# A mixture of experts in another order of steps: about three experts in flight instead of two

## The chip, the cores and the metric

The kernel runs on one core of one Trainium2 chip. The metric is the device time of one execution in microseconds (us), and the number to be predicted is the median of several runs of the changed kernel.

## The reference, cut to what matters

The program is a chain of two transformer blocks on 256 tokens of width 1024, all in float32. The change touches only the mixture of experts near the end of the second block, of which the reference is:

```python
def moe_swiglu(x, router_w, w1, w3, w2):
    """x: (B,S,D). Top-2 of 8 expert SwiGLU, gates = softmax over the selected logits."""
    ...
    logits = (xt @ router_w).astype(jnp.float32)
    top_vals, top_idx = lax.top_k(logits, TOP_K)
    gates = jax.nn.softmax(top_vals, axis=-1)
    ...
    for e in range(N_EXPERTS):
        out = out + combine[:, e:e + 1] * swiglu(xt, w1[e], w3[e], w2[e])
```

There are 8 experts. w1 and w3 of one expert are 1024 x 3584, its w2 is 3584 x 1024, so that the weights of all experts are 352 MB, and each is needed once. The 256 tokens take two experts each, 64 to an expert on average.

## The kernel before, in words

**Stages.** The attention blocks, a dense feed-forward layer and the router come first, up to about 805 us. Then the experts run until about 1700 us, then a small gated projection ends the kernel.

**Steps.** The hidden width of an expert is cut in four chunks (CHUNKS): three of 1024 columns, c = 0, 1, 2, and one of 512, c = 3. One step is one pair (expert, chunk). ORDER puts the experts as 0, 4, 1, 5, 2, 6, 3, 7, and STEPS sorts the pairs by 2 i + c, where i is the place in ORDER. So a steady stretch repeats chunk 0 of expert i, chunk 2 of expert i - 1, chunk 1 of expert i, chunk 3 of expert i - 1. The order of the weights in memory traffic follows the same list (_moe_steps, weights). A step with c = 0, 1 or 2 is called long below, one with c = 3 short.

**What a step does.** In experts(), each turn of the loop runs the w1 product of its chunk (result in the PSUM banks mm, then Silu to sw_s), its w3 product (banks s, then the product with sw_s), and the w2 product of the step before (banks o, added to the expert's results). A product is a call of wide(). It first does the first 64 tokens of the expert, with matmuls of 128 rows and 64 columns of the array. The tokens 65 to 96 and 97 to 128 (the function rest) are put off until the first weight part of the next product has run (catch_up). They stand under `with self.tc.If(many() > SET):` (line 1507) and a second, inner If (line 1510), so that their matmuls are in the program for every product but are jumped over where the expert has no more than 64 or 96 tokens. A weight part is given back only in rest, whether or not the If was taken.

**Between the parts.** The list mids puts other TensorE work between the parts of the w1 product, late between those of the w3 product:

- hidden, at part 2: transposes sw_s of the step before, for its w2 product (bank pair tr).
- gather, at parts 4 and 5: the inputs of the next expert, in the step just before its chunk 0 (`begin[x] == i + 1`). Its matmuls are tr<-oh,f. They write xT, a tile of inputs_T().
- turn of way_back, at part 6, and the four pieces of scatter at parts 2 to 5 of the w3 product: the results of an expert that has finished go back to its tokens. That is one step after the w2 product of its chunk 3.

**Weights.** _Stream loads weights in parts of 512 KB, in the order of use, from SyncE's queue (line 90). A part is loaded as soon as a slot is free: 8 wp, 10 in pool qp (EARLY), 6 in rp (MORE), 4 wh, 4 wl, 3 x and 1 gain make a ring of 36 slots, all tiles of 128 x 1024 floats. The first time round there are three more.

**Inputs and results.** inputs_T() and results() take their tiles of 512 KB from three buffers each (tags xh and xl of pool act).

Of the kernel before, what the change touches and what calls it, by code (L numbers as in the profile page):

```python
# [19 lines left out]
P = 128  # L20
# [3 lines left out]
KD = D // P  # L24
FF = 3584
FC = FF // 512
NE = 8
# [4 lines left out]
NC = len(CHUNKS)  # L32
# [2 lines left out]
BIG = 3e38  # L35

RAW = 8
EARLY = 10
MORE = 6
PARTS = 4  # L40
LAG = 2
# [5 lines left out]


ORDER = [e for e0 in range(NE // 2) for e in (e0, e0 + NE // 2)]
STEPS = [(ORDER[i], c) for _, c, i in sorted((2 * i + c, c, i) for i in range(NE) for c in range(NC))]  # L50


def _moe_steps():

    prev = None
    for e, c in STEPS:
        yield from (("w1", e, c), ("w3", e, c))
# [122 lines left out]
class _Direct:  # L180


    def __init__(self, net, stream):
        self.net = net
        self.plan = {c[0]: c for c in stream.plan}
        self.slot = (net.qp, "raw", EARLY)
        assert stream.loaded == len(stream.parts) and len(stream.parts) - stream.used <= stream.last
# [20 lines left out]
class _Net:  # L208
# [112 lines left out]
    def split(self, v, j=0, more=False):  # L321

        k, n = v.shape[1], v.shape[2]
        if more:
            wh, wl = (self.t(self.qp, [P, 1024], "raw", bufs=EARLY).bitcast(F32R) for _ in range(2))
        else:
# [1129 lines left out]

        return back, turn

    def inputs_T(self):
        return self.t(self.act, [P, KD, P], "xh", bufs=3)  # L1460

    def gather_tiles(self):
# [115 lines left out]

        self.wide(key, y, lhs, 512, many, take, mids)

    def results(self):
        return self.t(self.act, [P, 2, 512], "xl", bufs=3)

    def scatter(self, t, e, back, ys, many=None):
# [35 lines left out]
    def experts(self, sp, p, pp):  # L1620

        F = lambda f, *x: lambda: f(*x)
        tokens, xT, ys, back, gs = {}, {0: self.xg}, {}, {}, {}
        prev = done = None
        begin = {e: i for i, (e, c) in enumerate(STEPS) if c == 0}

        def number(e):

            if e not in tokens:
                tokens[e] = self.nc.values_load(self.counts[0:1, e : e + 1], engines=(mybir.EngineType.PE,), min_val=0, max_val=S)  # L1630
            return tokens[e]

        def turn_back(e):
            back[e], turn = self.way_back(sp, e)
            turn()

        def hidden_last(e, c, s):
            g = self.t(self.qp, [P, 1024], "raw", bufs=EARLY).rearrange("p (i q n) -> p i q n", i=2, q=4)
            gs[e, c] = self.hidden(sp, s, CHUNKS[c][1] // 2, g)

        def hidden(e, c, s):
            gs[e, c] = self.hidden(sp, s, CHUNKS[c][1] // 2)

        def finish(e, c, mids=None):

            if c == 0:
                ys[e] = self.results()
            self.down(("w2", e, c), ys[e], gs.pop((e, c)), CHUNKS[c][1] // 2, F(number, e), c == 0, mids)
            return e if c == NC - 1 else None

        for i, (e, c) in enumerate(STEPS):
            n = CHUNKS[c][1] // 2
            s = self.t(sp, [P, 2, 512], "sw_s")
            mids, late = {}, {}
            if i == 0:
                mids[2] = [self.begin]
            else:
                mids[2] = [F(hidden, *prev)]
            nx = [x for x in range(NE) if begin[x] == i + 1]
            if nx:  # L1660
                x = nx[0]
                oh = self.places(sp, x)
                xT[x] = self.inputs_T()
                for k in (0, 4):
                    mids.setdefault(4 + k // 4, []).append(F(self.gather, oh, xT[x], k))
            if done is not None:
                back[done], turn = self.way_back(sp, done)
                mids.setdefault(6, []).append(turn)
                late = {2 + 2 * t + k: [f] for t in range(NT) for k, f in enumerate(self.scatter(t, done, back[done], ys[done], F(number, done)))}
            if n < 512:  # L1670
                mids, late = ({k: m.get(2 * k, []) + m.get(2 * k + 1, []) for k in range(4)} for m in (mids, late))
            if i == len(STEPS) - 1:
                late[3] = [F(turn_back, e)]
                self.next_gain()
            self.up(("w1", e, c), xT[e], s, n, F(number, e), True, mids)
            self.up(("w3", e, c), xT[e], s, n, F(number, e), False, late)
            if i < len(STEPS) - 1:
                done = finish(*prev[:2]) if prev is not None else None
            else:
                finish(*prev[:2], {4: [F(hidden_last, e, c, s)]})  # L1680
            prev = (e, c, s)
            if i == len(STEPS) - 3:
                pT = self.ple_T(p)

        self.stream.wait()
        self.stream.advance(2)
        finish(*prev[:2])
        self.stream.advance(4)
        value = self.ple_value(1, pT, pp)
        self.play(value, n=1)  # L1690
        self.catch_up()
        self.sets.pop("s")
        ps = [[self.bank(tag) for _ in range(2)] for tag in ("tr", "s")]
        for t in range(NT):
            self.spread(ps[t], t, back[e], ys[e])
        with self.tc.If(number(e) > SET):
            for t in range(NT):
                self.spread_rare(ps[t], t, back[e], ys[e])
        return value, [F(self.add_gated, t, j, e, ps[t][j]) for t in range(NT) for j in range(2)]
# [153 lines left out]
    def moe(self, i):  # L1853
# [3 lines left out]
        value, done = self.experts(sp, p, pp)  # L1857
        x0, *x0T = (self.t(self.qp, [P, D], "raw", bufs=EARLY) for _ in range(3))
        x0T = [x.bitcast(F32R).rearrange("p (k n) -> p k n", k=KD) for x in x0T]
# [20 lines left out]
    def run(self, stop):  # L1880
# [8 lines left out]
        with ExitStack() as cx:  # L1889
# [7 lines left out]
            if n < stop:  # L1897
                self.qp = cx.enter_context(tc.tile_pool(name="sQ", bufs=1, reuse_waits="tile"))
                self.stream.more(self.qp, EARLY)
                self.mixer(1, *st, self.route_join, more, self.router_inputs)  # L1900
# [82 lines left out]
```

## Time and profile before

| what | value |
|---|---|
| median of 3 runs | 1743.54 us |
| lowest and highest | 1737.5 and 1758.56 us |
| the profiled execution | 1751.32 us |
| its span, first to last instruction | 1749.5 us |
| mean granted TensorE clock | 0.977 of full speed |
| TensorE (PE) busy | 1645.0 us, 94% |
| VectorE, ScalarE, GpSimd busy | 676.7, 513.9, 157.8 us |
| read from HBM | 486.60 MB |

The profiled execution is one run with the hardware profiler. What it spends outside its span is 1.8 us. All durations in the rows come from it, and the median of the runs lies 7.8 us under it. A busy PE is not a PE at its peak, since matmuls overlap.

### The profile page before, as it was taken

The numbers are of one execution on the slowest core, as the hardware profiler recorded it, in microseconds if no ns is written. First come the engines' busy times: TensorE is split into PE (matmuls) and PEld (weight loads), VectorE is DVE, ScalarE is ACT, GpSimd is POOL, SyncE is SP. The second block draws the span as 40 slices with busy tenths as digits, with TensorE's granted clock in tenths as the row PEclk, the third lists the DMA queues.
The fourth block names the chain that finished last, engine by engine and source line by source line (L and its number), as shares of the span: only waits on it lengthen the run. The fifth ranks groups of instructions, "written<-read, shape, count | busy, mean of one in ns | idle before, by whom it ended". The sixth has DMA issues, their size and how long they took to land. (4 is left out here: it accounts for less than half of the span.)

```text
span 1749.5 us, 24548 instructions
## 1 busy us (share of the span) xinstructions
PE 1645.0 (94%) x9749; PEld 1017.8 (58%) x9749; DVE 676.7 (39%) x1132; ACT 513.9 (29%) x840; POOL 157.8 (9%) x152
## 2 busy tenths in 40 slices
PE   8999999999999999999999998999998999989787
PEld 6887777787888877785334344345343353333336
DVE  6656767556544577663111201210211212112145
ACT  5646646555444455552000000000000000000013
POOL 2001433501000011420000000000000000000011
PEclk9999999889999999999999999999999999999998
DMA  8664325535555548748999999889999999999981
GB/s 274 199 183 146 111 86 163 193 103 175 177 190 192 192 157 293 235 164 353 406 403 406 406 398 357 341 346 343 348 378 368 377 406 389 401 407 404 402 302 67
DMA packets 176118, 491.71 MB, mean 281 GB/s; under 512 B 16670, under 2 KB 21206, under 8 KB 175920
## 3 DMA queue, kind: packets, MB, share of 16 engines
q1 hardware_dynamic: 171376, 474.28, 73.2%
q0 software_dynamic: 4544, 14.52, 2.8%
q8 instruction: 157, 2.57, 0.6%
q14 instruction: 41, 0.34, 0.1%
HBM read 486.60 MB, written 2.14 MB: 279 GB/s over the span
## 5 line engine op out<-in xcount | busy, mean ns | idle before, releaser
L282 PE MATMUL mm<-wh,xh 128*128 128x512 f32 (+5 forms) x996 | 325.0, 415 | 7.7 <-PEq L1507 2.4
L333 DVE TENSOR_TENSOR wl<-raw,wh 128x1024 fp32r<-128x1024 f32 x211 | 269.0, 1286 | 133.9 <-ACT wh L329 123.0
L282 PE MATMUL mm<-wh,xl 128*128 128x512 f32 (+1 forms) x700 | 279.7, 400 | 0.7 <-DVE xl L504 0.5
L329 ACT CAST wh<-raw 128x1024 fp32r<-128x1024 f32 x226 | 235.4, 1051 | 138.6 <-PE mm L282 67.1
L282 PE MATMUL mm<-wl,xh 128*128 128x512 f32 (+2 forms) x840 | 248.0, 422 | 3.5 <-PEq L1507 2.7
L282 PE MATMUL mm<-raw,xh 128*64 128x512 f32 (+3 forms) x1236 | 184.9, 475 | 13.0 <-PEq L1507 7.3
L1547 DVE TENSOR_TENSOR sw_s<-sw_s,s 128x512 f32<-128x512 f32 (+1 forms) x64 | 39.8, 621 | 402.6 <-PE s L282 366.8
L282 PE MATMUL o<-raw,sw_g 128*64 128x512 f32 (+1 forms) x1132 | 173.8, 501 | 16.0 <-PEq L1507 13.3
L282 PEld LDWEIGHTS mm<-wh,xh 128*128 128x128 f32 (+2 forms) x996 | 147.8, 171 | 54.3 <-issue 14.1
L282 PE MATMUL s<-raw,xh 128*64 128x512 f32 (+3 forms) x1016 | 158.7, 484 | 15.2 <-PEq L1507 6.9
L282 PEld LDWEIGHTS mm<-wl,xh 128*128 128x128 f32 (+2 forms) x840 | 141.1, 181 | 49.4 <-issue 13.5
L282 PEld LDWEIGHTS mm<-wh,xl 128*128 128x128 f32 x700 | 134.0, 191 | 29.5 <-DVE xl L504 2.5
L1560 ACT COPY sw_g<-tr 128x512 f32<-128x512 f32 (+1 forms) x31 | 16.6, 537 | 417.3 <-PE tr L285 417.3
L282 PEld LDWEIGHTS o<-raw,sw_g 128*64 128x64 f32 (+1 forms) x1132 | 64.8, 126 | 114.4 <-issue 74.4
L282 PEld LDWEIGHTS mm<-raw,xh 128*64 128x64 f32 (+1 forms) x1236 | 67.0, 127 | 107.7 <-issue 66.6
L282 PEld LDWEIGHTS s<-raw,xh 128*64 128x64 f32 (+1 forms) x1016 | 61.9, 130 | 104.7 <-issue 74.3
L1545 ACT ACTIVATE sw_s<-mm 128x512 f32<-128x512 f32 (+1 forms) x64 | 34.8, 544 | 198.7 <-PE mm L282 167.2
L1573 DVE TENSOR_TENSOR xl<-xl,o 128x512 f32<-128x512 f32 x48 | 32.9, 686 | 148.6 <-PE o L282 126.7
L310 POOL DMA_DIRECT2D gain<-in_ple_norm_g_dram x2 | 1.1, 558 | 860.0 <-DMA raw<-in_moe_w_dram 859.1
L331 POOL TENSOR_TENSOR wl<-raw,wh 128x1024 fp32r<-128x1024 f32 x15 | 37.9, 2545 | 402.5 <-ACT wh L329 382.5
L282 PE MATMUL s<-wh,xh 128*64 128x512 f32 (+6 forms) x364 | 58.8, 439 | 0.7 <-PEq L1507 0.3
L285 PEld LDWEIGHTS tr<-c_ident,sw_s 128*128 128x128 f32 x280 | 32.9, 147 | 30.8 <-issue 10.5
(387 smaller groups left out, 1786.1 us busy)
## 6 DMA issues: line engine op xcount, KB each, us to landing
raw<-in_moe_w_dram SPq DMA_DIRECT2D x454, 512.0 KB, 10.2
raw<-in_dense_w_dram SPq DMA_DIRECT2D x84, 512.0 KB, 4.5
wh<-in_moe_w_dram SPq DMA_DIRECT2D x72, 512.0 KB, 10.1
wl<-in_moe_w_dram SPq DMA_DIRECT2D x72, 512.0 KB, 10.1
x<-in_moe_w_dram SPq DMA_DIRECT2D x54, 512.0 KB, 10.1
raw<-in_w_in_dram SPq DMA_DIRECT2D x48, 512.0 KB, 4.6
raw<-in_nsa_w_in_dram SPq DMA_DIRECT2D x44, 512.0 KB, 5.1
gain<-in_moe_w_dram SPq DMA_DIRECT2D x17, 512.0 KB, 10.2
```

The lines of the kernel that those rows point to most:

```text
L282: self.nc.tensor.matmul(out, lhsT, rhs, start=start, stop=stop, **kw)
L285: self.nc.tensor.transpose(out, in_, self.ident if ident is None else ident)
L310: (eng or self.nc.gpsimd).dma_start(out, ap.partition_broadcast(P))
L329: self.nc.scalar.copy(wh, v)
L331: self.nc.gpsimd.tensor_tensor(wl, v, wh.bitcast(F32), ALU.subtract)
L333: self.owed.append(lambda: self.nc.vector.tensor_sub(wl, v, wh.bitcast(F32)))
L1545: nc.scalar.activation(s[:, i, :n], ps[i][:, :n], AF.Silu)
L1547: nc.vector.tensor_mul(s[:, i, :n], s[:, i, :n], ps[i][:, :n])
L1560: copy(g[:, i, : n // P, :], ps[:, :n].rearrange("p (q n) -> p q n", n=P))
L1573: self.nc.vector.tensor_add(ys[:, i, :], ys[:, i, :], y[i])
```

## The change

- STEPS sorts by 4 i + 3 c in place of 2 i + c. A steady stretch becomes chunk 0 of expert i, chunk 3 of expert i - 2, chunk 2 of expert i - 1, chunk 1 of expert i. So an expert is spread over ten steps in place of eight, and three are open at a time. The step list before begins (expert, chunk) (0,0) (0,1) (4,0) (0,2) (4,1) (0,3) (1,0) (4,2) (1,1) (4,3) (5,0); after, it begins (0,0) (0,1) (4,0) (0,2) (4,1) (1,0) (0,3) (4,2) (1,1) (5,0) (4,3). The last five steps are the same in both.
- EARLY goes from 10 to 8, so that the ring has 34 slots.
- Every fourth expert in ORDER takes its inputs and results from two new tiles, xh4 and xl4, in pool sE.

```diff
-EARLY = 10
+EARLY = 8
...
-STEPS = [(ORDER[i], c) for _, c, i in sorted((2 * i + c, c, i) for i in range(NE) for c in range(NC))]
+STEPS = [(ORDER[i], c) for _, c, i in sorted((4 * i + 3 * c, c, i) for i in range(NE) for c in range(NC))]
...
-    def inputs_T(self):
+    def inputs_T(self, i=0):
+
+        if i % 4 == 3:
+            return self.t(self.se, [P, KD, P], "xh4")
         return self.t(self.act, [P, KD, P], "xh", bufs=3)
...
-    def results(self):
+    def results(self, i=0):
+        if i % 4 == 3:
+            return self.t(self.se, [P, 2, 512], "xl4")
         return self.t(self.act, [P, 2, 512], "xl", bufs=3)
...
-                ys[e] = self.results()
+                ys[e] = self.results(ORDER.index(e))
...
-                xT[x] = self.inputs_T()
+                xT[x] = self.inputs_T(ORDER.index(x))
```

## Rows read from the trace of the kernel before

**Rows 1.** The page: busy time by engine (part 1), DMA queues (part 3).
```profile
PE 1645.0 (94%) x9749; PEld 1017.8 (58%) x9749; DVE 676.7 (39%) x1132; ACT 513.9 (29%) x840; POOL 157.8 (9%) x152
...
q8 instruction: 157, 2.57, 0.6%
```

**Rows 2.** Busy time by stretch: length, engines, PE clock share, DMA share, GB/s.
```profile
825.00:1060.00 235.00, 226.05 (x1593) 98.29 (x1589) 31.27 (x52) 19.24 (x34) 0.00 (x0) 0.99 1.03 404
1060.00:1450.00 390.00, 360.60 (x2963) 161.58 (x2962) 57.80 (x100) 25.08 (x46) 0.00 (x0) 0.98 0.94 361
1450.00:1675.00 225.00, 202.18 (x1027) 82.42 (x1025) 42.08 (x73) 18.03 (x33) 0.56 (x1) 0.98 1.03 403
```

**Rows 3.** Waits of SyncE's DMA queue, 805 to 1690 us: in total, times, longest.
```profile
SPq L90 <- DMA raw<-in_moe_w_dram: 254.9, 278, 2.0
SPq L90 <- PEq L1507: 116.1, 29, 11.4
```

**Rows 4.** Timeline of SyncE: issues into the one gain slot; the last expert loads.
```profile
902.37 0.33 SPq L90 DMA_DIRECT2D gain<-in_moe_w_dram  x1
...
1603.17 0.33 SPq L90 DMA_DIRECT2D gain<-in_moe_w_dram  x1
...
1675.97 5.34 SPq L90 DMA_DIRECT2D raw<-in_moe_w_dram  x5
```

**Rows 5.** Timeline of PE: the first use of the same tiles; the experts' last product.
```profile
920.36 1.06 PE L282 MATMUL o<-gain,sw_g 128*64 128x512 f32 x4
...
1622.47 1.06 PE L282 MATMUL o<-gain,sw_g 128*64 128x512 f32 x4
...
1697.17 2.79 PE L282 MATMUL o<-raw,raw 128*64 128x512 f32 x12 [0.15 <-PEq L1507]
```

**Rows 6.** DMA issues of the whole run: count, size, us from issue to landing.
```profile
gain<-in_moe_w_dram SPq DMA_DIRECT2D x17, 512.0 KB, 10.2
```

**Rows 7.** Instructions of line 1507: duration ns min/median/max; PE's timeline behind one.
```profile
L1507 PEldq COMPARE_BRANCH  x96: 65/422/7665, 810.3 to 1701.9; - x96
...
1651.56 1.82 PE L282 MATMUL mm<-raw,xh 128*64 128x512 f32 x4 [4.06 <-PEq L1507]
```

**Rows 8.** DMA queue of instructions: packets in 955:1440, 1440:1690 and 1624:1647.
```profile
q8 instruction: 60, 0.98, 0.8%
...
q8 instruction: 39, 0.64, 1.1%
...
q8 instruction: 4, 0.07, 1.2%
```

**Rows 9.** Timeline of PE: where steps start, and the moved work in them.
```profile
820.49 1.06 PE L282 MATMUL mm<-raw,xh 128*64 128x512 f32 x4
...
848.49 1.06 PE L282 MATMUL mm<-raw,xh 128*64 128x512 f32 x4
...
1526.11 1.06 PE L282 MATMUL mm<-x,xh 128*64 128x256 f32 x8
1529.34 3.84 PE L282 MATMUL tr<-oh,f 128*128 128x128 f32 x32
1549.81 1.06 PE L282 MATMUL mm<-raw,xh 128*64 128x512 f32 x4
...
1571.21 1.06 PE L282 MATMUL mm<-x,xh 128*64 128x512 f32 x4
1599.55 1.39 PE L282 MATMUL mm<-raw,xh 128*64 128x512 f32 x4
1624.18 1.06 PE L282 MATMUL mm<-raw,xh 128*64 128x256 f32 x8
1645.84 0.66 PE L285 MATMUL tr<-c_ident,p 128*128 128x128 f32 x4
1646.43 1.08 PE L282 MATMUL mm<-raw,xh 128*64 128x512 f32 x4
```

**Rows 10.** Timeline of PE: some of one product's matmuls for tokens past 64.
```profile
955.50 3.23 PE L282 MATMUL mm<-raw,xh 128*32 128x256 f32 x56
```

## The prediction

> **What bounds the kernel now.** I read the page first. TensorE is busy 94% of the span [rows 1], and no other engine comes near it, so the question is what TensorE waits for among the experts, the only stage that the change touches. Next comes the table by stretches [rows 2]. DMA moves 404 GB/s from 825 to 1060 us and 403 from 1450 to 1675, but 361 from 1060 to 1450, where its share falls to 0.94. The middle stretch holds 390 x (1 - 361/404) = 41.5 us in which DMA had nothing to do. SyncE's waits say why: 254.9 us for a load that is still under way, but also 116.1 us for line 1507, that is for slots that are given back only behind the If [rows 3]. So in the middle the ring is full and TensorE is the slower of the two; at both ends DMA runs without a break.
>
> That looks as if DMA bounded the ends and TensorE the middle, and a better mix would win back the 41.5 us. The next view decides it: does TensorE wait for weights at the ends? The gain tile is one slot of the ring and so a probe every 36 loads. It is issued at 902.37 and 1603.17 [rows 4], lands 10.2 us later [rows 6], and is first used at 920.36 and 1622.47 [rows 5]. The weights lay there for 17.99 - 10.2 = 7.8 us and 19.30 - 10.2 = 9.1 us, and these are the stretches in which the ring is emptiest. The last expert load is issued at 1675.97 + 5.34 = 1681.3 at the latest and lands at about 1691.5; the product that uses it runs from 1697.17. TensorE never runs out of weights. DMA at 404 GB/s is in time, and its idle 41.5 us cost nothing.
>
> What TensorE waits for at the ends is its own program. The compare-and-branch of line 1507 takes 0.07 us at the least and 7.67 at the most, and behind one of them PE stands still for 4.06 us [rows 7]. The instructions come through DMA in packets of 2.57 MB / 157 = 16 KB [rows 1, 8]. From 1440 to 1690 us, where the jumped-over matmuls are read in vain, there is one per 250/39 = 6.4 us; from 955 to 1440, where two experts execute theirs, one per 485/60 = 8.1 us [rows 8]. One expert of those runs both sets of matmuls for tokens past 64, 3.23 us for 56 of the 128 in one product [rows 10]. So a step of a light expert (at most 64 tokens) takes about as long as reading its program, a step of a heavy one as long as its matmuls.
>
> The short step shows it best. From 1624.18 to 1646.43 it takes 22.25 us with four such packets, 5.6 us each [rows 8, 9]. Its w1 and w3 products have half the columns but the same number of instructions as a long step's, so there is free time of TensorE in it.
>
> **The change part by part.** The profiled execution took 1751.3 us, 1.8 of them outside the span; the median of the runs is 7.8 us lower. I add the change to either.
>
> *Two slots fewer.* TensorE's start is not touched: the first loads land long before. DMA falls behind by two loads, 2 x 0.524 MB / 404 GB/s = 2.6 us. The cover is the 7.8 us at the emptiest probe, which leave 5.2. Between probes it can be less; I allow two us. Cost 0; without cover each missing us would cost one.
>
> *Heavy steps in other places.* The expert with two sets is third in ORDER. Its steps are number 7, 9, 12, 14 of 32 before and 6, 9, 12, 15 after; those of the other heavy one 15, 17, 20, 22 and 14, 17, 20, 23. Both kernels execute the same matmuls and read the same program. Heavy steps hardly come more evenly than before, and the DMA idle time stays within some us of 41.5. Cost 0.
>
> *The gather changes its host.* It comes just before a chunk 0. Before, six of the seven gathers sit in a short step (the one for expert 4 stays in step 2). After, these six sit in chunk 1 of the expert before, a long step. What it costs in either host is read from steps of light experts [rows 9]. Short with gather: 1549.81 - 1526.11 = 23.70 us. Short without: 22.25, less the foreign transposes at its end (1646.43 - 1645.84 = 0.59), so 21.66. The gather's 3.84 us of matmuls cost 2.04 there, the rest hides in the reading of the program. Long with gather: 848.49 - 820.49 = 28.00. Long without anything: 1624.18 - 1599.55 = 24.63. It costs 3.37 there, nearly all of it. So each move out of a light short step costs 1.33 us. Four of the six short steps are light; in the two heavy ones the matmuls of the later tokens are executed and the gather costs its whole length in both places. 4 x 1.33 = 5.3 us. Bounds: if the long step hid it all and the short one lost 2.04, -8 us (4 x 2.04); if the long step paid 3.84 six times and the short one gave nothing back, +23 us.
>
> A rule of the skill would give another sum. In the Trainium skill, Runtime: NRT & Kernel Launch, section "Instruction fetch mechanics", crossing into the next 16 KB of program is called mostly hidden, while a taken branch out of the window of two pages stalls. By its first half a short step would be as long as its matmuls, the gather would cost its length anywhere, and this term would be 0 and the time 1743.5, inside the spread of rival A. The four packets in 22.25 us speak against that half here, and the branch of 7.67 us for the other.
>
> *The scatter changes its host.* It comes one step after the w2 product of chunk 3: before in a chunk 2, after in a chunk 1, both long. It costs 1599.55 - 1571.21 = 28.34 us less 24.63, 3.71 in the one [rows 9] and the same in the other: 0. New is that gather, turn and hidden then share one w1 product and the two tr banks. Who is queued behind is the rest of that product. A bank must be copied out before its next user, and each waits at least one weight part. I know no row of the three together; 0 to 0.5 us each, six times, 0 to 3, and I take 0, as the copies run beside weight parts.
>
> *New tiles.* xh4 and xl4 are written once for each of two experts; before, a buffer came round after three experts, now four. No wait is added. Cost 0.
>
> Sum: +5.3 us. 1751.3 + 5.3 = 1756.6 against the profiled execution, 1743.5 + 5.3 = 1749 for the median.
>
> **The rivals.**
>
> A, the forecast: TensorE and its program bound the stage, 1749 us (1737 to 1757 with the spread of steps).
>
> B: a mix of three lets the program's reading run ahead in heavy steps and so shortens the light ones beside them. For it: a packet per 8.1 us where heavy steps run. Against: heavy steps are as many and as far apart as before. A plain long step takes 24.63 us; its three products of 32 matmuls, at 2.79/12 = 0.23 us each [rows 5], are 22.3. If a third of the other 2.3 us vanished in each of the 18 light long steps, -14 us: 1729.
>
> C: I misread the spare weights, and DMA's idle time is what counts. All of it regained, less the two slots: -41.5 + 2.6 = -39, 1705 us. Against: the weights that lie ready for 7.8 us and more at both ends.
>
> D, the other side: gather and scatter stacked in one long step are paid in full, and the short step stays at 23.7 us because four packets take their time whatever stands in it. Then the upper bound holds, +23 us: 1767. It decides for this if short steps without gather last over 23 us. For it: the packets of a step do not depend on the gather. Against: the short step of 22.25 us.
>
> E: the ring runs dry at one end, as 5.2 us of cover prove too few beside other delays; one stall of 6 to 10 us near one of the two probes: 1757 to 1759, say 1758.
>
> That the change does not do what it says, as heavy work lies where it lay, is part of A.
>
> **How the numbers follow.** A 0.62, B 0.15, C 0.04, D 0.14, E 0.05. The likeliest is 1749. The range leaves out C and the far ends of B and D: 1728 to 1768. About 2% is what a measurement of this kernel can tell from no change, its runs alone spread over 1.2%: 35 us, so under 1709 or over 1778. Faster by that: C, 0.04. Slower: D with more behind it, 0.04. Within: 0.92.
>
> **What would show it.** In the profile after, light short steps without gather should take some 22 us, chunk 1 steps with gather and scatter some 31 to 32; the gain tile should still lie ready for about 5 us at the emptiest; DMA between 1060 and 1450 should stay near 361 GB/s and the count of instruction packets at 157. I am wrong if PE waits for loads of moe weights by the tens of us, if the plain long step leaves 24.6, or if DMA's idle time and the time fall together.

## The result, and the profile after

| | before | after |
|---|---|---|
| median of 17 runs each | 1745.65 us | 1754.55 us |
| lowest to highest | 1737.5 to 1758.56 | 1747.69 to 1762.6 |
| the profiled execution (its span) | 1751.32 (1749.5) | 1753.85 (1752.0) |
| mean granted TensorE clock | 0.977 | 0.981 |

The ratio is 1.0064 [1.0047, 1.008]: the new order costs 8 to 14 us. The forecast was 1749, its range 1728 to 1768.

First, the page's rows for TensorE and for the instruction queue, against [rows 1]:

```profile
PE 1638.8 (94%) x9749; PEld 1011.1 (58%) x9749; DVE 674.9 (39%) x1132; ACT 514.3 (29%) x840; POOL 158.1 (9%) x152
...
q8 instruction: 157, 2.57, 0.6%
```

The same matmuls run, and the same 157 packets of program are read. The stretches, against [rows 2] (length, engines, PE clock, DMA share, GB/s):

```profile
825.00:1060.00 235.00, 220.53 (x1549) 92.99 (x1547) 31.46 (x52) 17.72 (x31) 0.00 (x0) 1.00 1.01 398
1060.00:1450.00 390.00, 359.86 (x2906) 161.55 (x2906) 59.04 (x101) 25.71 (x47) 0.00 (x0) 0.98 0.94 362
1450.00:1675.00 225.00, 200.88 (x1094) 83.28 (x1082) 42.78 (x75) 17.44 (x33) 0.56 (x1) 0.96 1.01 396
```

DMA still has idle time in the middle, 362 GB/s after 361. SyncE's waits between 805 and 1690 us say the same as [rows 3]:

```profile
SPq L90 <- DMA raw<-in_moe_w_dram: 261.6, 290, 2.4
SPq L90 <- PEq L1510: 106.1, 30, 10.5
```

Line 1510 is the If that was line 1507 before. The branch and its packets, against [rows 7, 8] (durations in ns; packets from 955 to 1440, then from 1440 to 1690 us):

```profile
L1510 PEldq COMPARE_BRANCH  x96: 65/426/6779, 797.5 to 1699.6; - x96
...
q8 instruction: 62, 1.02, 0.8%
...
q8 instruction: 38, 0.62, 1.0%
```

**Where the time went.** Cut both traces at TensorE's first expert matmul and at its first matmul of the projection behind the experts. In the timeline of PE these are, of the kernel after:

```profile
792.40 1.94 PE L282 MATMUL mm<-raw,xh 128*64 128x512 f32 x8
...
1695.59 0.50 PE L282 MATMUL mm<-wh,xh 128*128 128x512 f32 x1
```

and of the kernel before:

```profile
805.15 1.97 PE L282 MATMUL mm<-raw,xh 128*64 128x512 f32 x8
...
1699.89 0.50 PE L282 MATMUL mm<-wh,xh 128*128 128x512 f32 x1
```

| us | before | after | difference |
|---|---|---|---|
| front, up to the experts | 805.15 | 792.40 | -12.75 |
| stage, the experts | 894.74 | 903.19 | +8.45 |
| tail, behind them | 49.61 | 56.41 | +6.80 |
| span | 1749.5 | 1752.0 | +2.5 |

The front's difference isn't shown to be the change's: other profiled fronts are 792.6 us long with the old ring (e4, below) and 803.3 with the new one (e10). A window on 341.00 to 361.50 us shows what differed here. This is the row of before, and then that of after:

```profile
341.00:361.50 20.50, 20.50 (x70) 17.39 (x68) 6.22 (x9) 8.18 (x17) 7.41 (x7) 0.50 0.08 26
```

```profile
341.00:361.50 20.50, 20.50 (x135) 18.19 (x134) 12.80 (x17) 15.43 (x29) 7.13 (x7) 1.00 0.35 100
```

The profiled execution of before ran 20.5 us of it at a granted clock of 0.50 (1.2 GHz), that of after at 1.00 (2.4 GHz). TensorE did not idle in either row. So compare stages and tails, not spans: the two spans differ by 2.5 us where the medians differ by 8.9. One profile settles a stage to some us only: stage and tail together differ by 15.2 us here, the profiled execution of before lies 5.7 us above its median of 17, and those of e8, e9 and e10 below lie 12.7 above, 9.2 under and 12.0 above theirs.

The stage is longer by waits. These are its rows, of before and then of after:

```profile
805.15:1699.89 894.74, 829.75 (x5779) 358.14 (x5778) 145.16 (x258) 69.40 (x125) 2.91 (x2) 0.98 0.97 378
```

```profile
792.40:1695.59 903.19, 830.57 (x5780) 357.89 (x5779) 145.45 (x258) 71.83 (x127) 4.67 (x3) 0.98 0.97 379
```

TensorE is busy for 0.8 us more and idle for 72.6 us in place of 65.0.

**The tail** is the part that the prediction did not speak of. Here are rows of the kernel after: GpSimd, VectorE and TensorE around the end of the last product, and the clock:

```profile
1691.49 6.99 POOL L331 TENSOR_TENSOR wl<-raw,wh 128x1024 fp32r<-128x1024 f32 x3 [66.98 <-ACT wh L329]
...
1696.30 3.26 DVE L333 TENSOR_TENSOR wl<-raw,wh 128x1024 fp32r<-128x1024 f32 x1
...
1699.61 1.22 PE L282 MATMUL mm<-wl,xh 128*128 128x512 f32 x2 [2.82 <-DVE wl L333]
...
1699.30:1709.50 10.20, 9.18 (x20) 5.12 (x21) 3.74 (x6) 1.17 (x2) 0.00 (x0) 0.50 0.30 106
```

The projection's weights are split into a high and a low part, some low parts on GpSimd and some on VectorE. VectorE's takes 3.26 us here; GpSimd is at work until 1691.49 + 6.99 = 1698.48, and VectorE ends 1.08 us behind that, at 1699.56. In the trace of before the same subtraction began at 1700.60, when GpSimd was idle, and took 1.22 us. TensorE then waited 0.79 us for it, and here 2.82, after which the clock is at 0.50 (1.2 GHz) for 10.2 us. Over the whole tail the same 170 matmuls keep TensorE busy for 41.65 us at a mean clock of 0.81, against 37.51 at 0.88 before: 4.14 of the 6.80 us. The other 2.66 are waits.

The Trainium skill, SBUF — State Buffer, section "SBUF: two separate sides", says that GpSimd and a VectorE operation with two SBUF inputs share a pair of ports as an exclusive lock: whoever comes second stands still until the first has finished. The trace agrees, with the end 1.08 us behind GpSimd's.

### The profile page after: what moved, and what is told of

Same layout as the page of the kernel before. It is cut to its first block, busy times and chain, and to the rows that moved or that the text cites. A ratio compares the mean times of both kernels' runs of the same rounds, so it can differ in the third digit from the quotient of the medians.

```text
span 1752.0 us, 24531 instructions
## 1 busy us (share of the span) xinstructions
PE 1638.8 (94%) x9749; PEld 1011.1 (58%) x9749; DVE 674.9 (39%) x1132; ACT 514.3 (29%) x840; POOL 158.1 (9%) x152
## 5 line engine op out<-in xcount | busy, mean ns | idle before, releaser
L282 PE MATMUL mm<-wh,xh 128*128 128x512 f32 (+3 forms) x804 | 308.7, 426 | 3.7 <-DVE xl L504 1.9
L282 PE MATMUL mm<-wl,xh 128*128 128x512 f32 (+4 forms) x1080 | 264.9, 404 | 5.5 <-DVE wl L333 2.8
L282 PE MATMUL s<-raw,xh 128*32 128x256 f32 (+3 forms) x1360 | 175.7, 451 | 15.5 <-issue 4.6
L282 PE MATMUL mm<-raw,xh 128*64 128x512 f32 (+2 forms) x1084 | 174.9, 494 | 13.5 <-PEq L1510 7.7
L282 PEld LDWEIGHTS mm<-wl,xh 128*128 128x128 f32 (+2 forms) x1080 | 150.9, 169 | 58.9 <-issue 15.4
L282 PE MATMUL o<-raw,sw_g 128*64 128x512 f32 (+1 forms) x1072 | 163.5, 497 | 13.9 <-PEq L1510 9.2
L282 PEld LDWEIGHTS mm<-wh,xh 128*128 128x128 f32 (+2 forms) x804 | 140.0, 183 | 47.6 <-issue 14.3
L282 PEld LDWEIGHTS s<-raw,xh 128*64 128x64 f32 (+1 forms) x1360 | 73.5, 125 | 108.7 <-issue 72.1
L282 PEld LDWEIGHTS mm<-raw,xh 128*64 128x64 f32 (+1 forms) x1084 | 60.6, 130 | 93.9 <-issue 65.8
L282 PE MATMUL o<-wh,sw_g 128*128 128x512 f32 (+2 forms) x260 | 58.6, 476 | 0.1
## 6 DMA issues: line engine op xcount, KB each, us to landing
raw<-in_moe_w_dram SPq DMA_DIRECT2D x440, 512.0 KB, 10.2
wh<-in_moe_w_dram SPq DMA_DIRECT2D x76, 512.0 KB, 10.2
wl<-in_moe_w_dram SPq DMA_DIRECT2D x76, 512.0 KB, 10.2
x<-in_moe_w_dram SPq DMA_DIRECT2D x59, 512.0 KB, 10.2
gain<-in_moe_w_dram SPq DMA_DIRECT2D x18, 512.0 KB, 10.2
```

Of the source, the lines that this page charges most:

```text
L282: self.nc.tensor.matmul(out, lhsT, rhs, start=start, stop=stop, **kw)
```

## The experiments

Each is an edit of the kernel before or of the changed kernel, told as a short diff. "Stage" and "tail" are cut as above. The ratio is to the kernel before, run on the same chip.

| run | median us | ratio [95%] | stage | tail |
|---|---|---|---|---|
| before, after (profiles above) | 1745.65, 1754.55 | 1.0064 [1.0047, 1.008] | 894.7, 903.2 | 49.6, 56.4 |
| e1: order alone | 1755.34 | 1.0057 [1.0031, 1.0082] | 905.2 | 50.0 |
| e2: slots and tiles alone | 1747.87 | 1.0008 [0.9979, 1.0037] | 897.1 | 53.1 |
| e3: after, gathers in short steps | 1742.27 | 0.9988 [0.9962, 1.0014] | 889.7 | 56.4 |
| e4: before, six experts without the If | 1688.14 | 0.9684 [0.9646, 0.9722] | 841.4 | 49.7 |
| e5: after, the same | 1695.11 | 0.9728 [0.9702, 0.9754] | 847.6 | 49.3 |
| e6: before, gathers in chunk 1 | 1753.82 | 1.0059 [1.0035, 1.0082] | 900.3 | 50.0 |
| e7: after, scatters in chunk 0 | 1747.30 | 1.0018 [0.999, 1.0047] | 897.6 | 50.2 |
| e8: e3 with a ring of 35 | 1742.50 | 0.9984 [0.9966, 1.0002] | 896.0 | 52.8 |
| e9: after, gathers in chunk 2 | 1759.94 | 1.0089 [1.0057, 1.0121] | 903.6 | 51.4 |
| e10: e3 and e7 together | 1733.21 | 0.9936 [0.9911, 0.9961] | 883.3 | 56.9 |
| e11: e10, low parts on VectorE | 1726.66 | 0.9887 [0.9847, 0.9927] | 879.3 | 45.4 |
| e12: e11, six experts without the If | 1683.07 | 0.9637 [0.9619, 0.9655] | 840.2 | 45.3 |

**e1 and e2: the two halves of the change.** e1 is the kernel before with the new sort key alone; e2 is the changed kernel with the old key.

```diff
-STEPS = [... sorted((2 * i + c, c, i) ...)]
+STEPS = [... sorted((4 * i + 3 * c, c, i) ...)]
```

> The order of after alone: ring of 36 slots and the three buffers each for inputs and results as before. Theory G (the gather's host, as predicted): the experts' stage, from the first expert matmul to the first matmul of the projection behind them, is 5 us longer than before's 894.7 (near 900; after has 903), and the time is 5 us over before, ratio 1.003. Rival S (the two slots): the part behind the experts goes back from after's 56.4 us to before's 49.6 and the whole is as before, ratio 1.000.

> Before's order with after's ring of 34 slots and the two new tiles. Theory G: nothing is moved, the stage stays at 895 us and the ratio to before is 1.000. Rival S: the loads at the very end fall on other slots of the ring, so the last weights are cut at other times; the part behind the experts takes 56 us as in after instead of 49.6, ratio 1.004, with the stage unchanged.

The order alone gives the whole loss: stage +10.5, time 1.0057, about twice what theory G expected of it. Slots and tiles alone give nothing that can be measured (stage +2.4, time 1.0008), though their profile shows a tail that is 3.5 us longer.

**e3: the gathers back in the short steps.** In the changed kernel five of the gathers (not the two of the first steps) run two steps earlier, in chunk 3 of another expert.

```diff
-            nx = [x for x in range(NE) if begin[x] == i + 1]
+            nx = [x for x in range(NE) if begin[x] == (i + 3 if begin[x] > 5 else i + 1)]
```

> After, but with the gathers of five experts two steps earlier, in the short step, as before had them (the fourth tile holds the inputs). Theory G: three of these short steps are light, 1.33 us each come back, so 4 us under after: ratio to before 1.004 in place of 1.006, short light steps some 24 us and chunk 1 steps 3.4 us shorter. Rival S, and the rival that gather and scatter stacked are the cost only through the tr banks (0 to 3 us): no change from after or -3 us at most.

The stage falls by 13.5 us, to 5 us less than before, and the time to that of the kernel before. So where the gather stands is the cost, and it is larger than the expected 4 us.

Two steps show it. Below is chunk 1 of expert 5 in the changed kernel (its start, the gather's two halves, the start of the next step). Then follow chunk 3 of expert 5, from its start to the next step's, with its longest waits, and the start and end of chunk 3 of expert 6, a light step late in the stage:

```profile
1131.86 1.03 PE L282 MATMUL mm<-raw,xh 128*64 128x512 f32 x4
...
1136.94 2.05 PE L282 MATMUL tr<-oh,f 128*128 128x128 f32 x16
...
1139.93 2.05 PE L282 MATMUL tr<-oh,f 128*128 128x128 f32 x16
...
1163.56 1.06 PE L282 MATMUL mm<-raw,xh 128*64 128x512 f32 x4
...
1324.40 1.06 PE L282 MATMUL mm<-raw,xh 128*64 128x256 f32 x8
...
1337.98 3.81 PE L282 MATMUL s<-raw,xh 128*64 128x256 f32 x20 [2.95 <-issue]
...
1345.08 1.94 PE L282 MATMUL o<-raw,sw_g 128*64 128x512 f32 x8 [2.43 <-PEq L1510]
...
1351.11 1.06 PE L282 MATMUL mm<-wh,xh 128*64 128x512 f32 x4
...
1549.49 1.06 PE L282 MATMUL mm<-raw,xh 128*64 128x256 f32 x8
...
1571.74 1.86 PE L282 MATMUL mm<-wh,xh 128*64 128x512 f32 x6
```

The first two of these steps in e3:

```profile
1134.83 1.03 PE L282 MATMUL mm<-raw,xh 128*64 128x512 f32 x4
...
1162.27 1.06 PE L282 MATMUL mm<-raw,xh 128*64 128x512 f32 x4
...
1322.23 1.06 PE L282 MATMUL mm<-raw,xh 128*64 128x256 f32 x8
...
1329.39 3.84 PE L282 MATMUL tr<-oh,f 128*128 128x128 f32 x32
...
1336.78 2.81 PE L282 MATMUL s<-raw,xh 128*64 128x256 f32 x24 [0.81 <-PEq L1510]
...
1342.51 1.94 PE L282 MATMUL o<-raw,sw_g 128*64 128x512 f32 x8 [2.06 <-PEq L1510]
...
1348.54 1.06 PE L282 MATMUL mm<-wh,xh 128*64 128x512 f32 x4
```

The long step goes from 31.70 to 27.44 us: the gather cost 4.26 there, somewhat more than its matmuls, two halves of 2.05. The short step takes the gather in and does not grow: 26.71 without it, 26.31 with it. The rows of the two short steps, of after and of e3, say how:

```profile
1324.40:1351.11 26.71, 20.70 (x170) 11.49 (x168) 2.91 (x5) 1.36 (x3) 0.00 (x0) 0.94 1.03 408
```

```profile
1322.23:1348.54 26.31, 22.97 (x202) 13.91 (x200) 3.42 (x7) 2.52 (x5) 0.00 (x0) 1.00 1.03 407
```

And of the step in after, the stretch from the end of its longest wait on:

```profile
1337.50:1340.90 3.40, 2.92 (x14) 2.33 (x15) 0.00 (x0) 0.00 (x0) 0.00 (x0) 0.50 1.02 408
```

TensorE's idle time shrinks from 6.01 to 3.34 us, that is by 2.67: among it the waits of 2.95 and 2.43 us, which become 0.81 and 2.06. The second of them is for the If. The first is not, since it stands between two matmuls of one product and no branch lies in it; one packet of program is read meanwhile. The clock does the rest. In after it is at 0.50 (1.2 GHz) for 3.4 us from the end of that first wait on, and 20 matmuls of s take 3.81 us; in e3 it is at 1.00 throughout, and 24 take 2.81. Without the gather the step's matmuls take 22.97 - 3.84 = 19.13 us there, against 20.70. So the gather is hidden in waits for the program, and in this step also in the lower clock that followed one of them.

**e6 and e9: the gather in a long step, without a scatter beside it.** e3 alone leaves a rival open: gather and scatter share a product after the change, and might hold each other up. e6 puts the gather of the kernel before into chunk 1, where no scatter lies; e9 puts that of the changed kernel into chunk 2, likewise without one.

```diff
 e6, in the kernel before
-            nx = [x for x in range(NE) if begin[x] == i + 1]
+            nx = [x for x in range(NE) if begin[x] == (i + 2 if begin[x] > 2 else i + 1)]
 e9, in the changed kernel
-            nx = [x for x in range(NE) if begin[x] == i + 1]
+            nx = [x for x in range(NE) if begin[x] == (i + 2 if begin[x] > 5 else i + 1)]
```

> The kernel before, but six gathers run in chunk 1 of the expert before in place of the short step; order, ring and scatters as before, so gather and scatter lie in different steps. If the gather's host is the whole of the 13.5 us by which the experts' stage shrank when the changed kernel's gathers went back to short steps, this stage grows by 10 to 14 us from 894.7, to 905 to 909, and the time is some 1755. By the prediction's own term, 1.33 us for each of four light steps, it grows by 5.3, to 900, time 1749. If the stacking of gather and scatter in one step was the cost, and the host nothing, it stays at 895 and 1744.

> The changed kernel with the gather one step earlier, in chunk 2 of the expert before last, a long step that holds no scatter; the scatter stays in chunk 1. If a light long step pays for a gather in full wherever it stands (the prediction's rule), the stage stays at 900 to 905 us and the time at 1752 to 1757. If what costs is the gather beside the scatter, the stage falls as it did when the scatter was moved away, by 5 us or more to 894 to 898, and the time to 1745 to 1749.

In e6 the stage grows by 5.6 us, near the prediction's own 5.3; its time grows by more, 6 to 14 us, an interval that leaves 5.3 out. Summed over the timeline, the six long steps grow by 23.3 us (four of them by 4.26 or 4.27) and the six short ones shrink by 17.2. In e9 the stage stays at 903.6, as the rule of the long step has it; its median is even a little above after's and the range expected, with a ratio whose interval overlaps that of after. So the gather costs its length in a long step with or without a scatter.

**e7 and e10: the scatter one step later.** e7 is the changed kernel with the results of an expert sent back one step later: five of the scatters then lie in a chunk 0, that of expert 6 in a short step, chunk 3 of expert 3. e10 has the edit of e3 too.

```diff
-                done = finish(*prev[:2]) if prev is not None else None
+                done, held = held, finish(*prev[:2]) if prev is not None else None
+                if i == len(STEPS) - 2:
+                    done = held
```

> The changed kernel, but the results of an expert go back one step later, in a chunk 0, while the gather stays in chunk 1; nothing else moves. If gather and scatter stacked in one product cost the time, the stage falls from 903.2 by 8 us or more, to 895 or less, and the time to about 1746. If the gather's host alone is the cost, nothing changes but by some 2 us: stage 901 to 905, time 1752 to 1757.

> The changed kernel with the gathers in the short steps and the scatters in chunk 0, so that no step holds more than one of them. Stages so far: 903.2 changed, 889.7 with the gathers moved alone, 897.6 with the scatters moved alone. If the two gains are separate, the stage is 883 to 886 and the time 1734 to 1738, under both kernels. If both undo the same stacking, the second adds nothing: stage 888 to 892, time 1737 to 1743.

The same chunk 1 of expert 5, start and next start, in e7:

```profile
1139.95 1.03 PE L282 MATMUL mm<-raw,xh 128*64 128x512 f32 x4
...
1167.09 1.06 PE L282 MATMUL mm<-raw,xh 128*64 128x512 f32 x4
```

and in e10, where it holds neither:

```profile
1137.32 1.03 PE L282 MATMUL mm<-raw,xh 128*64 128x512 f32 x4
...
1160.20 1.06 PE L282 MATMUL mm<-raw,xh 128*64 128x512 f32 x4
```

The step takes 22.88 us empty, 27.14 with the gather, 27.44 with the scatter, and 31.70 with both. 22.88 + 4.26 + 4.56 = 31.70: the two add up to the last digit, and nothing is lost by stacking. In the other four chunk 1 steps that hold both, the same sum comes out to 0.07 us. The stage falls by 5.6 us in e7 all the same, to between the two ranges expected. Summed over the timeline, the five chunk 1 steps shrink by 30.0 us and the five chunk 0 steps behind them grow by 25.9. The sixth scatter takes 4.6 us from its long step and gives 5.2 to the short one, but the step behind that is 3.9 shorter. So the new hosts take the scatters for less; why a chunk 0 does so is not shown. In e10 the gains are separate, 13.5 + 5.6 = 19.1 expected and 903.2 - 883.3 = 19.9 found, and the kernel is under both, 0.9936 [0.9911, 0.9961].

**e4, e5 and e12: without the program that is jumped over.** In e4 and e5 the If and the matmuls for tokens past 64 are left out of the program for all experts but 1 and 2, the two that need them with these tokens. No executed matmul is missing with this input; with other inputs, experts with more than 64 tokens would lack them. e12 has the edit on top of e11.

```diff
-            with self.tc.If(many() > SET):
-                for j, (k0, k1, _, _) in parts:
-                    product(1, j, k0, k1)
+            if key[1] in (1, 2):
+                with self.tc.If(many() > SET):
+                    for j, (k0, k1, _, _) in parts:
+                        product(1, j, k0, k1)
...
```

> Before, with the matmuls for tokens past 64 and their branches left out of the program for the six experts that have no such tokens in this run. Theory P (reading the program bounds light steps, DMA does not): light short steps fall from 22 to 24 us to some 17 to 20 and long ones from 24.6 to 22.9 until DMA is the bound; DMA at 404 GB/s needs till about 1640 to 1665 for the expert weights, so the time falls by 35 to 55 us, ratio 0.97 to 0.98, and PE begins to wait for loads. Rival C (DMA bounds the ends already): at most 5 us less, ratio 0.997 to 1.000.

> The changed kernel, without the If and the matmuls for tokens past 64 of the six experts that have none such to run. The same edit in the kernel before gave 1688 us, with a stage of 841.4. If the new order costs only by work that the reading of the program no longer hides, its cost goes with that reading, and stages and times agree: 838 to 846 us and 1685 to 1695. If the mix of three experts is worth something once the loads bound the light steps, as heavy steps lie as they lay, that would show as a stage under 836. If the two slots fewer run the ring dry once the loads bound, the stage is 850 or more and PE waits for loads of weights by more than in that run.

> The kernel with gathers in short steps, scatters in chunk 0 and the splits on VectorE, without the If and the matmuls for tokens past 64 of the six experts that have none to run. The changed kernel with that edit alone had a stage of 847.6 us. With the If, the other places for gather and scatter took the stage from 903.2 to 883.3. If they gained because short steps and chunk 0 hide work in the reading of the program, nothing is left to hide in once it is gone: stage 843 to 850, time 1686 to 1692. If they gained by something else, such as banks or copies, the gain stays: stage 826 to 832, time 1668 to 1675.

Of e4: the page's row of the instruction queue, the stage, the branches that are left (now line 1508), and a row of PE in a light step late in the stage:

```profile
q8 instruction: 87, 1.43, 0.4%
...
792.56:1633.98 841.42, 814.35 (x5779) 333.93 (x5778) 142.15 (x259) 65.96 (x124) 0.56 (x1) 1.00 1.02 402
...
L1508 PEldq COMPARE_BRANCH  x24: 65/65/89, 928.3 to 1398.5; - x24
...
1538.23 1.08 PE L282 MATMUL s<-raw,xh 128*64 128x512 f32 x4 [0.18 <-DMA raw<-in_moe_w_dram]
```

With the same executed matmuls the stage is 53 us shorter. No branch of line 1508 takes over 89 ns, DMA moves 402 GB/s over the whole stage in place of 378, and late in the stage TensorE now waits some 0.2 us for a weight part: DMA has become the bound there. This is the plain proof that the light steps were waiting for their program.

Not all of the 53 us is waiting itself. TensorE's idle time falls from 65.0 to 27.1 us, that is by 37.9; the other 15.4 are its busy time, 829.75 us before and 814.35 here for the same matmuls. The granted clock of the stage was 0.98 before and is 1.00 here. One of the stretches at 0.50, of 3.4 us, begins at 1651.8 in the trace of before, right behind the wait of 4.06 us [rows 7].

The Trainium skill's "Instruction fetch mechanics" (Runtime: NRT & Kernel Launch), weighed in the prediction, calls crossing into the next 16 KB mostly hidden; in e4 the branches of the six experts and the reading of the program behind them are gone together, so these runs can't tell how the 53 us divide between the crossing and the branch. The wait of 2.95 us without a branch (e3, above) speaks against "mostly hidden" in that step.

In e5 the new order still costs 6.2 us of stage (847.6 against 841.4), so the first theory, by which its cost goes with the reading, does not hold in full; the ring's theory named 850 or more, which is not reached. In e12 the other hosts bring 847.6 to 840.2, 7.4 of the 19.9 us that they bring with the If; stage and time lie between the ranges of the two theories. So most of what hosts are worth hangs on the reading of the program, but not all. One short step shows the greater part plainly: chunk 3 of expert 0 takes 14.95 us in e5 (from 941.09) and 18.87 with the gather in e12 (from 939.89), 3.92 more, whereas with the If it takes 21.87 in after and 21.82 with the gather in e3. The rest may lie in light steps that now wait for loads; these runs don't settle it.

**e8 and e11: the tail.** e8 is e3 with EARLY = 9 and without xl4, a ring of 35 slots. e11 is e10 with the low parts of the projection's first gate weights on VectorE.

```diff
 e8
-EARLY = 8
+EARLY = 9
...
-        if i % 4 == 3:
-            return self.t(self.se, [P, 2, 512], "xl4")
 e11
-            self.net.aid = {("p", 1): (1,), ("pg", 1, 0): (0, 1, 2, 3), ...
+            self.net.aid = {("p", 1): (1,), ("pg", 1, 0): (), ...
```

> The changed kernel with the gathers in the short steps, and the one tile for results turned back into a weight slot, a ring of 35. If the tail behind the experts is longer after the change (56.4 us against 49.6) because the ring's round of 34 splits the projection's first loads, a ring of 35 gives another tail, 50 to 54 us, with a stage as with 34 (888 to 892), and a time of 1737 to 1741. If the tail hangs on the order of steps, it stays at 55 to 57 and the time at 1742.

> The kernel with the gathers in the short steps and the scatters in chunk 0, and the low parts of the projection's first gate weights are computed by VectorE in place of GpSimd. If the tail behind the experts is long (56.9 us there, 56.4 in the changed kernel, 49.6 before) because a subtraction of VectorE takes 3.3 us beside one of GpSimd in place of 1.2, and TensorE waits for it and then runs at half clock, the tail falls to 50 to 53 and the time to 1726 to 1730. If TensorE waits for these weights anyway, as there are more of them on one engine's queue, the tail stays at 55 or more and the time at 1733 or above.

e8 has a tail of 52.8 us, as expected of another ring, but its profiled stage (896.0) is longer than the expected 888 to 892 and its median no better than e3's: nothing to carry. e7 shows how little decides. It has after's ring of 34 and after's three splits of 6.99 us on GpSimd, here followed by VectorE's:

```profile
1690.80 6.99 POOL L331 TENSOR_TENSOR wl<-raw,wh 128x1024 fp32r<-128x1024 f32 x3 [69.81 <-ACT wh L329]
...
1697.72 1.22 DVE L333 TENSOR_TENSOR wl<-raw,wh 128x1024 fp32r<-128x1024 f32 x1
```

GpSimd is done at 1697.79, so VectorE's subtraction takes 1.22 us and the tail 50.2. In the changed kernel VectorE came 2.18 us too early for that, and the tail is 56.4. In e11 the collision is gone:

```profile
1680.18 3.49 DVE L333 TENSOR_TENSOR wl<-raw,wh 128x1024 fp32r<-128x1024 f32 x3
...
1681.46 0.73 PE L282 MATMUL mm<-wl,xh 128*128 128x512 f32 x2 [0.79 <-DVE wl L333]
```

Three subtractions take 3.49 us together, TensorE waits 0.79 us, and the tail is 45.4 us against e10's 56.9, less than the 50 to 53 that the first theory named; the time, 1726.66, is the one that it named. Of the kernels that compute all tokens of any input, e11 is the fastest: 0.9887 [0.9847, 0.9927]. e12, with its limit on the tokens, is at 0.9637 [0.9619, 0.9655].

## Why the prediction was right, and where it was mis-sized

**The bound.** Right: TensorE and the reading of its program, not DMA. e4 removes 70 of the 157 packets (157 - 87) and 53 us of stage.

**Two slots fewer, cost 0.** Right within the measurement: e2's time is 1.0008, with an interval of -0.2 to +0.4%. The emptiest probe of the ring, against [rows 4, 5], is the issue into the gain slot and its first use:

```profile
1599.33 0.33 SPq L90 DMA_DIRECT2D gain<-in_moe_w_dram  x1
...
1618.17 1.06 PE L282 MATMUL o<-gain,sw_g 128*64 128x512 f32 x4
```

18.84 us less 10.2 of flight leave 8.6 us, where about 5 were forecast. PE's waits in the trace of after do name loads, up to 4.5 us long, and a reader could take them for rival E. The longest late one for a part of a w1 product shows what they are (PE's timeline, then line 1510's instructions between 1640 and 1648 us):

```profile
1642.10 1.08 PE L282 MATMUL mm<-raw,xh 128*64 128x512 f32 x4
1647.27 1.18 PE L282 MATMUL mm<-raw,xh 128*64 128x512 f32 x4 [4.09 <-DMA wh<-in_moe_w_dram]
...
L1510 PEldq COMPARE_BRANCH  x1: 6077/6077/6077, 1641.0 to 1641.0; - x1
```

A branch of 6.08 us, from 1641.0 to 1647.1, stands in front of that matmul. The load is only the last semaphore event that the profile found. Of the six waits over 1 us that name a load, five have a branch of line 1510 in front of them, both of 4.5 us among these; the sixth, of 1.86 us at 863, has none. Rival E's stall of 6 to 10 us is not there.

**Heavy steps in other places, cost 0.** Not tried by itself. e3 has the old kind of host for the gather, another ring and the new order, and its stage is 5.0 us under before's:

```profile
796.20:1685.86 889.66, 825.02 (x5780) 356.29 (x5779) 145.34 (x258) 71.25 (x127) 2.63 (x2) 0.98 0.98 384
```

Its waits are as before, 64.6 us against 65.0; what is shorter is the busy time, 825.0 us against 829.8 for the same matmuls, and that hangs on the clock of one execution each. A gain of the order itself is not shown, and the median of e3 is that of before.

**The gather's host, +5.3 us.** The mechanism held and the size did not: this is the term that failed. Moving the gathers back in the new order is worth 13.5 us of stage. In the old order the stage agrees with the term, 5.6 in e6, but the median of e6 says 6 to 14. Its price of the long step was the difference of two unlike steps [rows 9]: one with a gather, the second of the stage, and one without, late in it, which takes 24.63 us because it waits for its program too. A long light step without either is shorter earlier on: 22.90 us in the trace of before (899.18 to 922.08), 22.88 in e10. It has almost no wait to hide anything in, and pays 4.26 for a gather and not 3.37. The five long steps of e3 shrink by 21.4 us together, 4.2 to 4.4 each. And the short steps of the new order take it for less than 2.04: -0.4 us in the step shown, 12.2 over all five, of which 6.4 come back in the step behind one of them, so 1.2 each. That leaves 15.6 us, of which other steps take back 2.1.

**The scatter's host and the stacking, cost 0.** The stacking costs nothing, to 0.01 us in the step shown. But the rule that any long step is as good as another was too coarse: the places one step later give back 5.6 us of stage, some 7 of median.

**What the sum lacked, and luck.** The tail, +6.8 us in the profile of after, is no part of any term. The experts end at another moment against the loads of the projection, and two engines collide. Its share of the median can't be told apart by these runs; e1, without it, shows the same loss as the change. That the forecast of +5.3 came within 4 us of the +8.9 between the medians is in part luck: the gathers that e3 moves back are worth 13.5 us of stage, over twice the one term, and the 5.0 us by which e3's stage is shorter than before's had no term either.

**The rivals.** B needed shorter plain steps; with 157 packets and DMA at 362 GB/s nothing ran ahead by an amount that shows. C is out: DMA's idle time is there after the change too, and goes only with the program (e4). D's condition was that light short steps without gather last over 23 us; late in the stage one takes 1571.74 - 1549.49 = 22.25. In the middle a short step lasts longer, 26.71 beside a heavy expert's product, but it hides the gather, so that there the mechanism of D was at work in part: the short step waited for its program, and the gather went into the waits. That fits a cost between A's 5.3 and D's 23.

**What was to be seen.** Chunk 1 with gather and scatter at 31 to 32 us: 31.70. Light short steps at some 22: 22.25. DMA near 361: 362. Packets: 157. One sign of being wrong was ill chosen: plain long steps of some 22.9 us, and not 24.6, are in the kernel before too.

## What to carry to other kernels

Price small work by the step that will host it, read from the same stretch of the trace: in a step that waits for its program a gather cost 1.2 us on average here, in one that TensorE fills its length and more. A list of steps is thus also a list of hosts, and the small pieces should be placed again when the steps are sorted anew; here that was worth 20 us of stage, while no gain of the order itself is shown. And look behind the stage too: the moment at which it ends decides which engines meet there.

## What the runs showed of the hardware

- Matmuls that are jumped over still cost their reading: leaving out 70 packets of 16 KB took 53 us from the stage, 37.9 of them waits and 15.4 busy time at a granted clock of 0.98 that became 1.00, and the If's longest compare-and-branch went from 7665 ns [rows 7] to 89 ns.
- Pieces that share a product with others add up exactly: 22.88, 27.14, 27.44 and 31.70 us for none, gather, scatter and both. A gather of two halves of 2.05 us costs 4.26 in place.
- VectorE's subtraction of 1.22 us took 3.26 beside one of GpSimd, ending 1.08 us behind it, and the 2.82 us for which TensorE then waited were followed by 10.2 us at a granted clock of 0.50.
